# Norms' sums of squares, a positional term and weight low parts change engines in a two-layer decoder trunk

## The chip, the core and the metric

One core of a Trainium2 chip runs the whole program. The metric is device time in microseconds (us), the median of several executions. The engines are TensorE (PE for matmuls, PEld for its weight loads), VectorE (DVE), ScalarE (ACT), GpSimd (POOL) and SyncE (SP), whose queue issues the DMAs. Each has its own in-order queue, and semaphores order them.

## The reference

Two decoder layers on 256 tokens of width 1024, float32 throughout. Layer 0 mixes tokens by native sparse attention ("nsa"), layer 1 by differential attention ("diff").

```
for layer in (0, 1):
    x = x + 0.5 * swiglu(rmsnorm(x, ffn1_norm), ffn1_w_in, ffn1_w_out)      # 1024 -> 2 x 2816 -> 1024
    x = x + mixer(rmsnorm(x, mix_norm))                                     # 0: nsa, 1: diff
    x = x + 0.5 * swiglu(rmsnorm(x, ffn2_norm), ffn2_w_in, ffn2_w_out)
rmsnorm(x, g) = x * rsqrt(mean(x * x) + 1e-6) * g
# in nsa: overlapping blocks of 32 tokens, stride 16, become one token each through an MLP
blocks = concat(sub[:, :, 0:15], sub[:, :, 1:16])                           # sub: 16 tokens x 64 per head
kc, vc = gelu((blocks + pos) @ w1) @ w2                                     # pos: 32 x 64, for kc and for vc
# in diff: two softmaxes of one head are subtracted, p0 - lambda * p1, and multiply v
```

## The kernel before

Every product of float32 numbers is made of three TensorE products: both factors are split into a high part (a rounded copy) and a low part (the number less its high part), and high x high, high x low and low x high are summed in PSUM (`mm3`, `mm3x`; in the FFN one matmul of 512 columns and one of 256). Activations lie transposed, channels in partitions, in `xT`.

The weights come through the class `Stream`. A list of chunks of 128 x 2048 numbers (1 MB) is loaded in the order of use into three raw buffers by SyncE (`_load`); `_piece` splits 512 columns at a time: ScalarE writes the high part (L86), then VectorE (L89), GpSimd (L91) or both write the low part. `Stream.pool` is the share of each piece's low part that goes to GpSimd. It is 0 in the FFNs, `NSA_SPLIT` = 0.875 in the head loop of nsa (448 of 512 columns), `DIFF_SPLIT` = 1 in the head loop of diff and `TAIL_SPLIT` = 1 just after it. `pump` splits ahead of use, by at most two chunks.

`Norm` makes what the next stage multiplies with. For each of four banks, `parts` writes the scaled high and low parts `xhl` (L327 on ScalarE, L328 on VectorE), and `squares` squares the bank on ScalarE (L334) and adds it into `acc` on GpSimd (L336, and L338 for the last fold). `rms_row` (the FFNs) multiplies `acc` with a matrix of ones on TensorE (L352), which gives every partition the sum over channels, and takes the reciprocal root on VectorE in eight steps over 256 columns. `rms` (the mixers) does it with two columns. In the first FFN `rms_row` stands after the last k step of block 0, and the evacuation `evac(0)` (the SwiGLU product, split into `hh` and `hl`) after step 3 of block 1; in the other FFNs they stand after steps 6 and 1.

In `nsa`, the projection "kc" leaves compressed keys and values in two banks, tokens in partitions. ScalarE scales them into `kcn` and writes each twice side by side (L627). During the next projection `kc_t` transposes them four heads at a time (L637), and VectorE copies each bank out in two halves of 64 partitions while it adds the positional term (L641), which lies as a column per partition in `gcol`. Then `kcs` is the split of `kc2`, and `mlp` multiplies with it (L680, L682) in between the steps of the projection "q0".

In `diff`, the head loop runs eight heads two ahead: `qk` (L1075), `chain` (the biased scores on VectorE, L548, and the exponential on ScalarE, L549; the bias is made on GpSimd, L1062), `mid` (L1095 to L1102 on VectorE: the two softmaxes are normalised and subtracted) and `tr` (the transposes of the result, L1109). Between them `fill` hands out steps of a generator, `filler`: the projections dk1, dq1, dv0 and dv1, the products with v of the first heads (`pv`), a norm of each pair of heads (`sub_b`: L992 to L1007) and half of the output projection. How many steps stand where is written out in `DIFF_FILL`. The order of the instructions on each engine is set by a scheduler when the program is built, from priorities in the order of the source and a table of costs; `tc.high_priority` lifts the lines under it. The order on the chip is therefore not the order of the source in detail.

Of the kernel before, what the change touches and what calls it, by code (L numbers as in the profile page):

```python
# [10 lines left out]
F32 = mybir.dt.float32  # L11
# [6 lines left out]
P = 128  # L18
# [105 lines left out]
def trunk_kernel(ctx, tc, x, ffn1_norm, ffn1_w_in, ffn1_w_out, mix_norm, ffn2_norm, ffn2_w_in, ffn2_w_out,  # L124
# [38 lines left out]
    rows_b = t3("rows_b", P)[:40]  # L163
# [90 lines left out]
    def setup_late():  # L254
        for i, g in enumerate((mix_norm, ffn2_norm)):
            nc.sync.dma_start(rows_a[16 + 16 * i:32 + 16 * i, :], g.rearrange("l (k p) -> (l k) p", p=P))
        nc.sync.dma_start(cst[:, P:], consts[:, P:])
        for c in range(2):
            cs = slice(c * DH, (c + 1) * DH)
            nc.sync.dma_start(rows_b[0:1, cs], nsa_q_norm)  # L260
            nc.sync.dma_start(rows_b[1:4, cs], nsa_k_norm[0])
            nc.sync.dma_start(rows_b[4:5, cs], diff_q_norm)
            nc.sync.dma_start(rows_b[5:6, cs], diff_k_norm)
            for kv in range(2):
                nc.sync.dma_start(rows_b[8 + 16 * kv:24 + 16 * kv, cs], nsa_cmp_pos[0, kv, 16 * c:16 * c + 16, :])
        nc.sync.dma_start(rows_b[6:7, :], diff_subln)
        nc.sync.dma_start(rows_b[7:8, :], diff_subln)
        nc.sync.dma_start(w2sb, nsa_cmp_w2[0].rearrange("v (c p) d -> p v c d", p=P))

    def setup_late2(b):  # L270
        nc.tensor.transpose(b[:, :48], rows_a, ident[:48, :48])
        nc.vector.tensor_copy(gcol[:, 16:48], b[:, 16:48])
        nc.tensor.transpose(b[:, 64:104], rows_b, ident[:40, :40])
        nc.vector.tensor_copy(gcol[:, 48:88], b[:, 64:104])
# [3 lines left out]

    posT = gcol[:, 56:88].rearrange("p (v i) -> p v i", v=2)
# [31 lines left out]
    class Norm:  # L311
# [19 lines left out]
        def squares(self, b):  # L331
            xb = xT[:, 2 * b:2 * b + 2, :].rearrange("p k t -> p (k t)")
            sq = self.acc if b == 0 else t2("sq")
            nc.scalar.activation(sq, xb, AF.Square)  # L334
            if b:
                nc.gpsimd.tensor_tensor(self.acc, self.acc, sq, op=ALU.add)  # L336
            if b == 3:
                nc.gpsimd.tensor_tensor(self.acc[:, :S], self.acc[:, :S], self.acc[:, S:], op=ALU.add)  # L338

        def rms(self, ps):  # L340
# [7 lines left out]
            rsqrt(v, 2, self.r)  # L348

# [23 lines left out]
    def ffn(nrm, nxt_g, last=False, first=False):  # L373
# [7 lines left out]
        def stage1(p):  # L381
            for half in range(2):
# [3 lines left out]
                for kk in range(4):  # L386
# [13 lines left out]
                    if p == 0 and k == (7 if first else 6):  # L400
                        nrm.rms_row(B[2])
                    if p == 1 and k == (3 if first else 1):
                        evac(0)
# [210 lines left out]
    DIFF_FILL = [(2, 5), (2, 6), (1, 3), (1, 3), (1, 3), (1, 3), (1, 1), (1, 0)]  # L614
    NSA_SPLIT = 0.875
    DIFF_SPLIT = 1.0
    TAIL_SPLIT = 1.0

    def nsa(nrm, nxt_g):
# [6 lines left out]
        for tb in range(2):  # L626
            nc.scalar.activation(kcn[:, tb], halves(B[4 + tb], 8).unsqueeze(2).to_broadcast([P, 8, 2, DH]), AF.Copy,  # L627
                                 scale=r[:, tb:tb + 1])
# [5 lines left out]
        def kc_t(kv, tb):  # L634
# [5 lines left out]
            for rows, o0, o1, n0 in ((slice(0, DH), 8 * tb, 8 * tb + 8, 0), (slice(DH, P), 8 * tb - tb, 7 + 8 * tb, 1 - tb)):  # L640
                nc.vector.tensor_tensor(dst[rows, :, o0:o1], src[rows, :, n0:n0 + o1 - o0],  # L641
                                        posT[rows, kv, None, None, :].to_broadcast([DH, HKV, o1 - o0, 16]), op=ALU.add)
# [96 lines left out]
        for k in proj("q0", nrm, full(0), (4, 4)):  # L739
            next(m)  # L740
# [198 lines left out]
    def diff(nrm, nxt_g):  # L939
# [82 lines left out]
        def filler():  # L1022
# [14 lines left out]
            for k in proj("dv1", nrm, full(2), (4, 4)):  # L1037
                if k in (2, 5):
                    pv(k // 3, B[k // 3])
                if k in (4, 7):  # L1040
                    next(subs[k // 6])
                yield
            v_ev(1, 2)
            for g in subs:
                next(g)
# [80 lines left out]
        for h in range(2):  # L1126
            qk(h)
            chain(h)
            fill(2)
# [38 lines left out]
    for b in range(4):  # L1168
# [4 lines left out]
        nrm.parts(b, halves(B[b], 2))  # L1173
        W.pump(1, 512)
    W.pump(4, 512)
    for b in range(4):
        nc.vector.tensor_copy(xT[:, 2 * b:2 * b + 2, :].rearrange("p k t -> p (k t)"), B[b])
        nrm.squares(b)
# [36 lines left out]
```

## Time and profile before

| | us |
|---|---|
| median of 3 executions (1073.1 to 1074.43) | 1073.56 |
| the profiled execution, device time | 1074.49 |
| its span, first to last instruction | 1072.5 |
| PE busy in the span | 1040.3 (97%) |
| DVE busy | 797.1 (74%) |
| ACT busy | 615.5 (57%) |
| POOL busy | 143.1 (13%) |

Each stage shows in the profile as a stretch: the first FFN to about 202 us, nsa to 380, two FFNs to 757, diff to 890, the last FFN to the end. A wait is shown with what ended it ("<-"), and the idle time of an engine that is not the bound costs nothing.

### The profile page before, as it was taken

The numbers are of one execution on the slowest core, as the hardware profiler recorded it, in microseconds if no ns is written. First come the engines' busy times: TensorE is split into PE (matmuls) and PEld (weight loads), VectorE is DVE, ScalarE is ACT, GpSimd is POOL, SyncE is SP. The second block draws the span as 40 slices with busy tenths as digits, with TensorE's granted clock in tenths as the row PEclk, the third lists the DMA queues.
The fourth block names the chain that finished last, engine by engine and source line by source line (L and its number), as shares of the span: only waits on it lengthen the run. The fifth ranks groups of instructions, "written<-read, shape, count | busy, mean of one in ns | idle before, by whom it ended". The sixth has DMA issues, their size and how long they took to land.

```text
span 1072.5 us, 17582 instructions
## 1 busy us (share of the span) xinstructions
PE 1040.3 (97%) x6486; PEld 915.2 (85%) x6486; DVE 797.1 (74%) x1762; ACT 615.5 (57%) x1397; POOL 143.1 (13%) x168
## 2 busy tenths in 40 slices
PE   8999999989899999999999999999979899999998
PEld 6899999879676899999999999999857698888887
DVE  7876766889797796766779676677987867676674
ACT  6564555658487665555566455556647556565552
POOL 2000000100544010000000000001268542000000
PEclk9999999999899999999999999999989899999999
DMA  7756555378410266565565655546533435556551
GB/s 239 242 171 211 178 194 196 120 157 252 147 41 1 79 197 212 178 200 190 164 197 162 212 179 194 194 160 202 159 116 101 136 93 183 196 162 217 185 183 39
DMA packets 129970, 178.02 MB, mean 166 GB/s; under 512 B 5162, under 2 KB 104668, under 8 KB 129884
## 3 DMA queue, kind: packets, MB, share of 16 engines
q1 hardware_dynamic: 129708, 176.84, 51.4%
q8 instruction: 50, 0.82, 0.3%
q14 instruction: 36, 0.29, 0.1%
q10 hardware_dynamic: 176, 0.07, 0.0%
HBM read 175.84 MB, written 1.05 MB: 165 GB/s over the span
## 4 chain that ended last, share of the span: by engine, by line
PE 84%; DVE 10%; ACT 2%; issue 2%; DMA 1%; POOL 0%; SPq 0%; DVEq 0%; ACTq 0%; POOLq 0%
PE bank L396 27%; PE bank L398 14%; PE bank L359 7%; PE bank L360 6%; PE bank L361 6%; PE bank L364 6%; PE bank L365 6%; PE bank L366 6%; DVE wlo L89 3%; PE bank L920 1%; PE bank L901 1%; DVE kc L641 1%; DMA xnat<-in_x_dram 1%; PE bank L1075 1%; ACT p L549 1%
## 5 line engine op out<-in xcount | busy, mean ns | idle before, releaser
L89 DVE TENSOR_TENSOR wlo<-raw,whi 128x512 fp32r<-128x512 f32 (+1 forms) x623 | 402.2, 686 | 129.8 <-ACT whi L86 128.7
L86 ACT CAST whi<-raw 128x512 fp32r<-128x512 f32 x667 | 373.2, 618 | 200.8 <-PE bank L396 121.8
L396 PE MATMUL bank<-xhl,whi 128*128 128x512 f32 x1280 | 451.1, 394 | 0.0
L398 PE MATMUL bank<-xhl,wlo 128*128 128x256 f32 x1280 | 361.5, 282 | 0.0
L396 PEld LDWEIGHTS bank<-xhl,whi 128*128 128x128 f32 x1280 | 240.5, 188 | 54.1 <-DVE ab L418 0.2
L398 PEld LDWEIGHTS bank<-xhl,wlo 128*128 128x128 f32 x1280 | 240.7, 188 | 0.4
L364 PE MATMUL bank<-hh,whi 128*128 128x256 f32 x528 | 149.4, 283 | 1.1 <-ACT hh L424 1.1
L365 PE MATMUL bank<-hh,wlo 128*128 128x256 f32 x528 | 149.3, 283 | 0.0
L366 PE MATMUL bank<-hl,whi 128*128 128x256 f32 x528 | 149.2, 283 | 0.0
L416 DVE TENSOR_TENSOR ab<-bank,sh 128x256 f32<-128x256 f32 x160 | 60.2, 417 | 72.9 <-ACT sh L415 72.9
L415 ACT COPY sh<-bank 128x256 f32<-128x256 f32 x160 | 55.9, 374 | 94.3 <-PE bank L398 94.2
L336 POOL TENSOR_TENSOR acc<-acc,sq 128x512 f32<-128x512 f32 x18 | 28.6, 1590 | 596.7 <-ACT sq L334 596.0
L364 PEld LDWEIGHTS bank<-hh,whi 128*128 128x128 f32 x528 | 101.0, 191 | 2.6 <-ACT hh L424 1.4
L365 PEld LDWEIGHTS bank<-hh,wlo 128*128 128x128 f32 x528 | 101.0, 191 | 0.0
L366 PEld LDWEIGHTS bank<-hl,whi 128*128 128x128 f32 x528 | 101.0, 191 | 0.0
L91 POOL TENSOR_TENSOR wlo<-raw,whi 128x512 fp32r<-128x512 f32 (+1 forms) x60 | 75.5, 1286 | 110.9 <-ACT whi L86 108.4
L359 PE MATMUL bank<-whi,xhl 128*128 128x512 f32 (+1 forms) x192 | 77.4, 403 | 0.0
L360 PE MATMUL bank<-wlo,xhl 128*128 128x512 f32 (+1 forms) x192 | 75.4, 393 | 0.0
L361 PE MATMUL bank<-whi,xhl 128*128 128x512 f32 (+1 forms) x192 | 74.6, 389 | 0.0
L418 DVE TENSOR_TENSOR ab<-ab,rb 128x512 f32<-128x512 f32 x80 | 54.5, 681 | 0.0
L549 ACT ACTIVATE p<-p,mn 128x128 f32<-128x128 f32 (+1 forms) x96 | 42.9, 451 | 18.6 <-DVE mn L548 18.4
L424 ACT CAST hh<-sh 128x256 fp32r<-128x256 f32 x88 | 34.9, 399 | 19.4 <-DVE sh L422 19.4
(249 smaller groups left out, 1438.4 us busy)
## 6 DMA issues: line engine op xcount, KB each, us to landing
raw<-in_ffn_w_in_dram SPq DMA_DIRECT2D x174, 512.0 KB, 4.9
raw<-in_ffn_w_out_dram SPq DMA_DIRECT2D x44, 1024.0 KB, 5.0
raw<-in_diff_w_in_dram SPq DMA_DIRECT2D x12, 1024.0 KB, 5.2
raw<-in_nsa_w_in_dram SPq DMA_DIRECT2D x6, 1024.0 KB, 6.0
raw<-in_nsa_cmp_w_dram SPq DMA_DIRECT2D x8, 512.0 KB, 5.2
raw<-in_nsa_w_out_dram SPq DMA_DIRECT2D x4, 1024.0 KB
raw<-in_diff_w_out_dram SPq DMA_DIRECT2D x4, 1024.0 KB, 5.1
raw<-in_nsa_w_in_dram SPq DMA_DIRECT2D x4, 512.0 KB
```

What stands on the lines that cost most here:

```text
L86: self.nc.scalar.copy(hi[:, a:b], raw[:, a:b])
L89: self.nc.vector.tensor_tensor(lo[:, a:m], raw[:, a:m], hi[:, a:m].bitcast(F32), op=ALU.subtract)
L91: self.nc.gpsimd.tensor_tensor(lo[:, m:b], raw[:, m:b], hi[:, m:b].bitcast(F32), op=ALU.subtract)
L359: nc.tensor.matmul(ps, wh, xh, start=start, stop=False, skip_group_check=True)
L360: nc.tensor.matmul(ps, wh, xl, start=False, stop=False, skip_group_check=True)
L361: nc.tensor.matmul(ps, wl, xh, start=False, stop=stop, skip_group_check=True)
L364: nc.tensor.matmul(ps, wh, xh, start=start, stop=False, skip_group_check=True)
L365: nc.tensor.matmul(ps, wl, xh, start=False, stop=False, skip_group_check=True)
L366: nc.tensor.matmul(ps, wh, xl, start=False, stop=stop, skip_group_check=True)
L396: nc.tensor.matmul(g, wh, nrm.both[:, k].rearrange("p c t -> p (c t)"), start=k == 0, stop=False, skip_group_check=True)
L398: nc.tensor.matmul(g[:, :S], wl, nrm.hi[:, k, :], start=False, stop=k == KT - 1, skip_group_check=True)
L416: nc.vector.tensor_tensor(ab[j][:, cs], g[:, :S], sh[j][:, cs], op=ALU.add)
```

## The change

Three things change. (1) `squares` adds on VectorE; in the first FFN, whose input arrives with tokens in partitions, ScalarE squares the input itself and sums along the row (`squares_nat`), VectorE takes the reciprocal root of two columns and writes it on the diagonal of a matrix (`rms_nat`), and TensorE spreads it with the ones (`row_nat`); that row and `evac(0)` then stand where they stand in the other FFNs. (2) The positional term is loaded with tokens in partitions, repeated eight times over 16 tokens (`posn`, eight DMAs in place of four), and is added as the bank is scaled, on VectorE; the copies out of the transposes add nothing, and of their two halves one is ScalarE's. (3) The three shares are 0, so that VectorE makes every low part. With it the places of filler steps move: `DIFF_FILL`, three steps instead of two after each of the first two heads, the order of `pv` and `sub_b` in dv1, and the steps of `mlp` in q0, which start one later.

```diff
+    posn = bp.tile([P, HQ, S], F32, tag="qT", bufs=1, name="posn")[:, 0].rearrange("p (v c d) -> p v c d", v=2, c=2)
...
-            for kv in range(2):
-                nc.sync.dma_start(rows_b[8 + 16 * kv:24 + 16 * kv, cs], nsa_cmp_pos[0, kv, 16 * c:16 * c + 16, :])
+        for n in range(P // 16):
+            nc.sync.dma_start(posn[16 * n:16 * n + 16].rearrange("l v c d -> l (v c) d"),
+                              nsa_cmp_pos[0].rearrange("v (c l) d -> l (v c) d", l=16))
...
             if b:
-                nc.gpsimd.tensor_tensor(self.acc, self.acc, sq, op=ALU.add)
+                nc.vector.tensor_tensor(self.acc, self.acc, sq, op=ALU.add)
             if b == 3:
-                nc.gpsimd.tensor_tensor(self.acc[:, :S], self.acc[:, :S], self.acc[:, S:], op=ALU.add)
+                nc.vector.tensor_tensor(self.acc[:, :S], self.acc[:, :S], self.acc[:, S:], op=ALU.add)
...
+        def squares_nat(self, src, half):
+            if half == 0:
+                self.ss = tiny("xss", 4)
+            for tb in range(2):
+                i = 2 * half + tb
+                nc.scalar.activation(t2("junk"), src[:, tb, half * 512:(half + 1) * 512], AF.Square, accum_out=self.ss[:, i:i + 1])
+        def rms_nat(self):
+            v = tiny("v", 2)
+            nc.vector.tensor_tensor(v, self.ss[:, 0:2], self.ss[:, 2:4], op=ALU.add)
+            nc.vector.tensor_scalar(v, v, -0.5 / D, -0.5 * EPS, op0=ALU.mult, op1=ALU.add)
+            r = rsqrt(v, 2)
+            self.diag = t2("diag", S)
+            for tb in range(2):
+                nc.vector.tensor_scalar(self.diag[:, tb * P:(tb + 1) * P], ident, r[:, tb:tb + 1], None, op0=ALU.mult)
+        def row_nat(self, ps):
+            nc.tensor.matmul(ps[:, :S], ones, self.diag, start=True, stop=True)
+            self.rb = xp.tile([P, S], F32, tag="rb", bufs=1, name=nm("rb"))
+            nc.vector.tensor_copy(self.rb, ps[:, :S])
...
-                    if p == 0 and k == (7 if first else 6):
-                        nrm.rms_row(B[2])
-                    if p == 1 and k == (3 if first else 1):
+                    if p == 0 and k == 6:
+                        (nrm.row_nat if first else nrm.rms_row)(B[2])
+                    if p == 1 and k == 1:
                         evac(0)
...
-    DIFF_FILL = [(2, 5), (2, 6), (1, 3), (1, 3), (1, 3), (1, 3), (1, 1), (1, 0)]
-    NSA_SPLIT = 0.875
-    DIFF_SPLIT = 1.0
-    TAIL_SPLIT = 1.0
+    DIFF_FILL = [(2, 4), (1, 4), (2, 2), (1, 3), (1, 3), (1, 3), (1, 1), (1, 0)]
+    NSA_SPLIT = 0
+    DIFF_SPLIT = 0
+    TAIL_SPLIT = 0
...
-        for tb in range(2):
-            nc.scalar.activation(kcn[:, tb], halves(B[4 + tb], 8).unsqueeze(2).to_broadcast([P, 8, 2, DH]), AF.Copy,
-                                 scale=r[:, tb:tb + 1])
+        for kv in range(2):
+            hs = slice(kv * HKV, (kv + 1) * HKV)
+            for tb in range(2):
+                for c in range(2):
+                    nc.vector.scalar_tensor_tensor(kcn[:, tb, hs, c, :], halves(B[4 + tb], 8)[:, hs, :], r[:, tb:tb + 1],
+                                                   posn[:, kv, None, c, :].to_broadcast([P, HKV, DH]), op0=ALU.mult, op1=ALU.add)
...
-                nc.vector.tensor_tensor(dst[rows, :, o0:o1], src[rows, :, n0:n0 + o1 - o0],
-                                        posT[rows, kv, None, None, :].to_broadcast([DH, HKV, o1 - o0, 16]), op=ALU.add)
+                (nc.scalar.copy if n0 != 0 or o0 < 8 * tb else nc.vector.tensor_copy)(dst[rows, :, o0:o1], src[rows, :, n0:n0 + o1 - o0])
...
         for k in proj("q0", nrm, full(0), (4, 4)):
-            next(m)
+            if k:
+                next(m)
+            if k == KT - 1:
+                next(m)
...
             for k in proj("dv1", nrm, full(2), (4, 4)):
+                if k in (1, 4):
+                    pv(k // 4, B[k // 4])
                 if k in (2, 5):
-                    pv(k // 3, B[k // 3])
-                if k in (4, 7):
-                    next(subs[k // 6])
+                    next(subs[k // 5])
+                if k == 6:
+                    next(subs[0])
                 yield
             v_ev(1, 2)
-            for g in subs:
-                next(g)
+            next(subs[1])
...
             chain(h)
-            fill(2)
+            fill(3)
         mid(0)
...
         nrm.parts(b, halves(B[b], 2))
+        if b % 2:
+            nrm.squares_nat(x_nat, b // 2)
         W.pump(1, 512)
+    nrm.rms_nat()
     W.pump(4, 512)
-    for b in range(4):
+    for b in (2, 0, 1, 3):
         nc.vector.tensor_copy(xT[:, 2 * b:2 * b + 2, :].rearrange("p k t -> p (k t)"), B[b])
-        nrm.squares(b)
```

The row block `rows_b` shrinks from 40 rows to 8 with it, and the copy of its transpose in `setup_late2` from 40 columns to 8.

## Rows read from the trace of the kernel before

**Rows 1.** The page, part 1: busy time, share of the span, instructions.
```profile
PE 1040.3 (97%) x6486; PEld 915.2 (85%) x6486; DVE 797.1 (74%) x1762; ACT 615.5 (57%) x1397; POOL 143.1 (13%) x168
```
**Rows 2.** Waits of PE, longest in total first: total us, times, longest.
```profile
PE bank L1109 <- DVE p L1102: 6.5, 2, 6.3
PE bank L352 <- POOL acc L338: 3.3, 2, 1.7
PE bank L722 <- DVE ck L713: 3.0, 1, 3.0
PE bank L359 <- DVE ol L1005: 2.3, 1, 2.3
...
PE bank L1002 <- DVE on L999: 1.7, 1, 1.7
...
PE bank L680 <- DVE kcs L645: 1.3, 1, 1.3
PE bank L364 <- ACT hh L424: 1.1, 1, 1.1
PE bank L682 <- DVE wlo L89: 0.9, 2, 0.6
PE bank L637 <- DVE kc L641: 0.7, 1, 0.7
```
**Rows 3.** Stretches: us, busy us of PE, PEld, DVE, ACT, POOL; granted clock; DMA.
```profile
60.00:202.00 142.00, 142.00 (x946) 130.60 (x945) 96.00 (x189) 75.49 (x164) 0.00 (x0) 1.00 0.57 185
770.00:850.00 80.00, 69.50 (x340) 51.91 (x338) 66.79 (x167) 46.57 (x122) 57.59 (x67) 0.95 0.38 119
850.00:890.00 40.00, 39.65 (x304) 37.97 (x303) 28.77 (x69) 21.32 (x46) 18.53 (x13) 0.92 0.35 113
```
**Rows 4.** The same view, short stretches behind the two long waits of diff.
```profile
790.00:795.00 5.00, 5.00 (x14) 3.92 (x13) 2.44 (x3) 3.46 (x7) 1.68 (x2) 0.54 0.51 189
...
850.00:855.00 5.00, 4.94 (x19) 3.66 (x17) 4.70 (x13) 0.46 (x2) 1.67 (x2) 0.50 0.40 119
```
**Rows 5.** Timelines of DVE, POOL and PE, 764 to 800: start, us, instruction.
```profile
782.85 5.63 DVE L1100 TENSOR_SCALAR p<-p,f 128x128 f32<-128x128 f32 x2
...
799.21 0.28 DVE L1100 TENSOR_SCALAR p<-p,f 128x128 f32<-128x128 f32 x1
...
783.20 4.94 POOL L91 TENSOR_TENSOR wlo<-raw,whi 128x512 fp32r<-128x512 f32 x4
...
782.01 0.39 PE L360 MATMUL bank<-wlo,xhl 128*128 128x512 f32 x1
782.24 0.39 PE L361 MATMUL bank<-whi,xhl 128*128 128x512 f32 x1
788.91 0.89 PE L1109 MATMUL bank<-cst,p 128*128 128x128 f32 x2 [6.28 <-DVE p L1102]
```
**Rows 6.** Groups by line and form, DVE and POOL, 770 to 890: count, busy us, mean ns.
```profile
L1100 DVE TENSOR_SCALAR p<-p,f 128x128 f32<-128x128 f32 x8 | 9.6, 1202 | 0.1
L89 DVE TENSOR_TENSOR wlo<-raw,whi 128x512 fp32r<-128x512 f32 x12 | 8.0, 714 | 0.0
...
L306 DVE TENSOR_TENSOR ra<-ra,dv 128x4 f32<-128x4 f32 x4 | 2.7, 666 | 0.0
...
L91 POOL TENSOR_TENSOR wlo<-raw,whi 128x512 fp32r<-128x512 f32 x44 | 56.0, 1303 | 46.9 <-ACT whi L86 46.8
```
**Rows 7.** The same view over the whole span.
```profile
L91 POOL TENSOR_TENSOR wlo<-raw,whi 128x448 fp32r<-128x448 f32 x16 | 19.5, 1240 | 64.0 <-ACT whi L86 61.6 <-ACT oh L922 2.4
...
L641 DVE TENSOR_TENSOR kc<-bank,gcol 64x512 f32<-64x512 f32 x6 | 6.4, 1072 | 0.1
...
L328 DVE SCALAR_TENSOR_TENSOR xhl<-bank,gcol,xhl 128x256 fp32r<-128x256 f32 x8 | 3.8, 480 | 1.6 <-ACT xhl L327 1.4
```
**Rows 8.** Timelines of DVE at the start and of POOL at 886.
```profile
19.49 8.47 DVE L89 TENSOR_TENSOR wlo<-raw,whi 128x512 fp32r<-128x512 f32 x8
...
886.09 5.12 POOL L336 TENSOR_TENSOR acc<-acc,sq 128x512 f32<-128x512 f32 x1 [2.89 <-ACT sq L334]
```

More of the change, by code (lines that the diff above doesn't have):

```diff
@@ L162, in trunk_kernel @@
     rows_a = t3("rows_a", P)[:48]
-    rows_b = t3("rows_b", P)[:40]
+    rows_b = t3("rows_b", P)[:8]
+    posn = bp.tile([P, HQ, S], F32, tag="qT", bufs=1, name="posn")[:, 0].rearrange("p (v c d) -> p v c d", v=2, c=2)
     gcol = cp.tile([P, 96], F32, name="gcol")
@@ L272, in setup_late2 @@
         nc.vector.tensor_copy(gcol[:, 16:48], b[:, 16:48])
-        nc.tensor.transpose(b[:, 64:104], rows_b, ident[:40, :40])
-        nc.vector.tensor_copy(gcol[:, 48:88], b[:, 64:104])
+        nc.tensor.transpose(b[:, 64:72], rows_b, ident[:8, :8])
+        nc.vector.tensor_copy(gcol[:, 48:56], b[:, 64:72])
         nc.vector.tensor_scalar(gk[:, :3], gcol[:, 49:52], gcol[:, 48:49], -0.125, op0=ALU.mult, op1=ALU.mult)
@@ L277, in setup_late2 @@
         nc.vector.tensor_scalar(gsub, gcol[:, 54:55], 1.0 - lam_init, None, op0=ALU.mult)
-    posT = gcol[:, 56:88].rearrange("p (v i) -> p v i", v=2)
     def load_lambda():
```

## The prediction

> **What bounds the kernel now.** I read the shares of busy time first. TensorE is busy for 97% of the span [rows 1], and in the FFNs without a gap: 142.00 of 142.00 us in the stretch from 60 to 202, with VectorE at 96 and GpSimd at 0 [rows 3]. The change leaves TensorE's work as it is, so nothing can be won there. What can be won is the 32.2 us in which TensorE isn't busy (1072.5 less 1040.3), and the time in which it runs at its lower clock. So the second view is what TensorE waited for, longest in total [rows 2]. Three families stand out: waits for `acc` from GpSimd (3.3 us), waits around the compression in nsa (L637, L680, L682: 2.9 us), and waits in the head loop of diff (L1109, L1002, L359: 10.5 us). The third view is the stretches: from 770 to 850 TensorE lacks 10.5 of 80 us while GpSimd is busy for 57.59 [rows 3]. Just behind the two long gaps of diff the granted clock is 0.54 and 0.50, the lower of its two levels, 1.2 of 2.4 GHz [rows 4]. With 5 us each that is (1 - 0.54) x 5 + (1 - 0.50) x 5 = 4.8 us more.
>
> The fourth view, the timeline, tells why. VectorE started a pair of L1100 at 782.85 and needed 5.63 us; a single one of the same form took 0.28 us at 799.21. In those 5.63 us GpSimd ran four low parts back to back, 783.20 to 788.14, and TensorE's transposes started at 788.91, right behind [rows 5]. So the VectorE instruction was held while GpSimd worked, and TensorE paid 6.28 us for it. The groups of 770 to 890 show it as a rule: L1100 takes 1202 ns in the mean, and L306, four numbers per partition, 666 [rows 6]. It goes the other way too: one GpSimd addition took 5.12 us at 886 [rows 8].
>
> **The change part by part.**
>
> *Low parts to VectorE in diff.* 44 pieces leave GpSimd (56.0 us) [rows 6]. On VectorE one costs 8.0/12 = 0.67 us, or a little less where pieces follow each other and overlap; with 0.62, 44 x 0.62 = 27.3 us. Against it stands what VectorE no longer loses. L1100 alone loses 9.6 - 8 x 0.28 = 7.4 us [rows 5, 6]. Nineteen groups of that stretch, from L1100 (128x128) to L306, are stretched in the same way; at the shortest time of each form they lose about 33 us together. GpSimd keeps what is not L91, mostly biases: 57.59 + 18.53 - 56.0 = 20 us, a quarter of its time there [rows 3, 6]. So I take 27 of the 33 as won; the bounds are 10 and 33. The additions of the norm bring 3 x 0.67 + 0.4 = 2.4 us. VectorE's load from 770 to 890 is then 66.79 + 28.77 + 27.3 + 2.4 - 27 = 98 us, about what it was.
>
> What happens to the gap at 782? The four pieces that GpSimd ran there, and four before them, are 8 x 0.62 = 5 us on VectorE ahead of the chain; the stretched steps before 782 and VectorE's idle moments pay for most of that. L1100 itself gets 5 us shorter, so L1102 should end near 785. TensorE reaches the transposes later: two more filler steps stand ahead of them, of six matmuls of 512 columns, 0.23 us apart [rows 5], 2.8 us together, so near 785.3. I leave 0.5 of 6.5 us (bounds 0 and 3). The waits at L1002 and L359 (4.0 us) come from `sub_b`, a row of tiny steps stretched like L306, and `dv1` now starts it earlier. I leave 1.0 of 4.0. With the gaps the low clock behind them goes (4.8). Since VectorE is loaded for 98 us in a stage of some 106, some head will wait that doesn't now: I add 2.0 (bounds 0 and 10). Sum: -(6.5 + 4.0 + 4.8) + 0.5 + 1.0 + 2.0 = -11.8 us.
>
> *Low parts in nsa.* 16 pieces of 448 columns [rows 7] go to VectorE, where 16 stumps of 64 columns become full pieces: below 16 x 0.67 = 11 us, and VectorE loses stretching there too. The wait for L722 (3.0 us) sits on a chain of small steps that the low parts stretch and delay; four of them were GpSimd's and now stand in VectorE's queue at that place. I count 0; bounds -7 (with the low clock behind it, taken as in diff) and +2.
>
> *Sums of squares.* On GpSimd an addition takes up to 5.12 us [rows 8], on VectorE 0.67. At the start the sum now comes from the input itself, no longer through copies, squares, three additions and a fold: half of the 3.3 us goes. VectorE gets some 12 tiny steps ahead of the low parts of the second chunk, at an estimated 0.2 us (L306 without its stretching) 2.5 us. Against that, eight low parts took 8.47 us there beside GpSimd's additions, where 8 x 0.62 is 5 [rows 8], and eight steps of 256 columns disappear. ScalarE's squares move into its pause before the last half of the input; the second pair may push its first weight pieces by under a microsecond. With `evac(0)` two steps earlier the wait for `hh` (1.1 us) goes. In the last FFN the wait for `acc`, the other half of 3.3, goes: its last addition needed those 5.12 us. At the other norms no wait stands; VectorE's adds there are paid for by an unstretched L328. Sum: -(3.3 + 1.1) = -4.4 us, bounds -4.4 and -2.
>
> *Positional term.* VectorE gains 8 instructions of 128 x 256 out of PSUM, 480 ns by the nearest row (L328, bank) [rows 7], about 3.5 us in a row, in part in idle time. It loses 8 x 1.07 us (L641) and gets four copies of half the partitions. These cost between 0.67 (a plain piece of 512 columns) and 1.07 us (L641, if the strided write is what is slow) [rows 6, 7]; I take 0.9, between them. ScalarE loses two instructions and gets the other four copies. The two halves then run side by side, so `kcs` is ready before TensorE gets there, all the more as the first step of `mlp` starts one step of q0 later: the 1.3 goes, and the 0.9. The first bank is freed no earlier than now, since the eight scalings stand before it; I leave the 0.7 [rows 2]. Gain 2.2 us, bounds 0 and 2.9. Eight DMAs instead of four pass SyncE's queue in the third block of the first FFN, among the weight loads. Three raw buffers give those loads a lead of two chunks, which hides them; without it TensorE would wait for the four, a microsecond or two.
>
> **The skill against the trace.** VectorE was held for a run of four GpSimd instructions [rows 5]. The Trainium skill ("SBUF — State Buffer", "SBUF: two separate sides") says that the two engines share a pair of ports as an exclusive lock, which the first to start keeps for its whole instruction. Taken by the letter, a hold lasts one instruction; that is rival F. Another page speaks against the change: the Trainium skill, "Perfetto Trace Analysis", "Optimizing Scalar/DVE Operations", lets a saturated VectorE offload work, even to GpSimd, though it warns that between these two it may not help. That is rival B.
>
> **How the numbers follow.** -11.8 - 4.4 - 2.2 = -18.4 us. Against the profiled execution, 1074.49 us, that is 1056.1; the median of the runs, 1073.56, is 0.9 us lower, so 1055.2: I say 1055.
>
> A. *Forecast*, 1050 to 1059: 47%.
>
> B. *VectorE becomes the bound, slower.* Place: the head loop of diff. If the long L1100 and L306 aren't GpSimd's doing, VectorE has 24.4 us idle from 770 to 890 [rows 3] and gets 27.3 + 2.4: at least 5 us more, and each of eight heads waits behind two pieces, 1.2 us, another 10. The gaps of diff stay; 6.6 us are won elsewhere: 1073.6 + 15 - 6.6 = 1082. It decides if less than a third of the 33 us comes back. For it: 98 of 106 us even by my count. Against: rows 5. 6%.
>
> C. *New waits eat half.* VectorE's order puts pieces before the chain, or GpSimd's biases are now held by VectorE's runs, as the addition at 886 was: one more us at each of eight heads and one more stretch at the low clock, 8 + 2.4: 1065. 20%.
>
> D. *The wait for L722 goes as well*, with its low clock, 7 us: 1048. 17%.
>
> E. *The gaps only move* under the scheduler's new order: 1073. 5%.
>
> F. *GpSimd holds VectorE for one instruction only*, 4.94/4 = 1.24 us; the rest of the 6.28 has another cause and stays, 1055.2 + 6.28 - 1.24 - 0.5 = 1059.7: 5%. Against it: four instructions fill the hold to the end.
>
> Faster by more than 0.2% (2.1 us, about what a measurement of this kernel tells from none): A, C, D and F, 0.89; within it E, 0.05; slower B, 0.06. The range takes in A, C, D and F and the bounds of the new waits: 1044 to 1067.
>
> **What would show it.** After the change L1100 (128x128) should take about 0.3 us and L306 0.2; no wait of TensorE for `acc`; the wait for L1102 under 1 us; no stretch at half clock in the head loop of diff; VectorE at about 0.9 there; L91 gone. If L1100 stays above 0.9 us, the mechanism is wrong. If it shrinks and TensorE still lacks 10 us in diff, it is C.

## The result, and the profile after

The changed kernel takes 1048.18 us (median of four executions, 1047.14 to 1048.75) against 1073.33 us of the kernel before beside it: ratio 0.9765, 95% interval 0.9748 to 0.9782. That is 25 us faster, inside the predicted range, 7 us below the predicted 1055, and the time that rival D gave (1048). The profiled execution took 1047.14 us in all, with a span of 1045.4.

The page of the kernel after, part 1, answers [rows 1].

```profile
PE 1028.2 (98%) x6486; PEld 906.8 (87%) x6486; DVE 779.2 (75%) x1834; ACT 618.4 (59%) x1403; POOL 39.5 (4%) x84
```

TensorE has the same 6486 matmuls, and yet is busy for 12.1 us less (1040.3 before). That is the clock: its mean granted value was 0.987 in the profiled execution before and is 1.000 after. The time in which TensorE isn't busy fell from 32.2 to 17.2 us, by 15.0. The two sum to the 27.1 us between the spans. VectorE took over 60 low parts and is busy for 18 us *less*, standing still included. With the low parts alone moved it is 8 less (789.2 us, run e1 below), and with the other steps alone also 18 less (779.1, run e2).

TensorE's waits after, longest in total first (total us, times, longest), answer [rows 2]. In the new source L1139 is the old L1109, L1132 the old L1102, L1130 the old L1100, L383 to L385 the old L359 to L361, L748 the old L722.

```profile
PE bank L1201 <- DMA xnat<-in_x_dram: 3.1, 2, 2.7
PE bank L1194 <- DVE warm L1192: 1.6, 1, 1.6
PE bank L1139 <- DVE p L1132: 1.3, 1, 1.3
PE bank L894 <- DVE mn L572: 1.1, 1, 1.1
PE bank L383 <- ACT oh L1033: 0.8, 1, 0.8
```

The waits for `acc`, `ck` and `kcs` are gone, and of the wait for L1102 in diff 1.3 is left of 6.5. The longest wait is now for the input itself, which no step of the change touches.

To see where the time went, I cut both spans at the same TensorE instructions: the first matmul of block 1 of the first FFN, the first transpose of `kcn`, the first matmul of the second FFN's block 1, the first `qk` of diff and the first block-1 matmul of the last FFN. Stretches of the kernel before, then of the kernel after (length, busy us of PE, PEld, DVE, ACT, POOL, granted clock, DMA): start, rest of the first FFN, nsa, diff.

```profile
0.00:25.40 25.40, 20.16 (x119) 16.58 (x120) 17.64 (x27) 17.26 (x33) 6.08 (x10) 0.93 0.79 251
25.40:221.91 196.51, 195.40 (x1255) 177.35 (x1254) 142.74 (x284) 109.20 (x234) 5.29 (x5) 1.00 0.60 187
221.91:383.38 161.47, 151.95 (x991) 124.79 (x989) 137.46 (x424) 107.78 (x289) 44.11 (x65) 0.97 0.37 110
774.89:894.83 119.94, 107.48 (x641) 89.06 (x641) 93.65 (x235) 64.30 (x160) 74.20 (x77) 0.94 0.38 122
```

```profile
0.00:22.00 22.00, 17.29 (x117) 14.58 (x118) 15.10 (x38) 14.21 (x31) 0.51 (x6) 1.00 0.85 280
22.00:217.16 195.16, 195.16 (x1257) 177.51 (x1256) 141.99 (x290) 110.84 (x239) 0.44 (x1) 1.00 0.61 192
217.16:370.09 152.93, 146.88 (x990) 121.25 (x989) 131.05 (x424) 111.25 (x292) 21.17 (x45) 1.00 0.39 115
761.61:867.50 105.89, 103.56 (x641) 86.04 (x641) 87.10 (x276) 64.56 (x160) 17.36 (x32) 1.00 0.40 130
```

Each row splits into busy time (the same matmuls, so what falls there is the clock, give or take the two matmuls that changed sides in the first rows) and the rest, the gaps:

| stretch | gained | of it gaps | of it TensorE's busy time |
|---|---|---|---|
| start | 3.4 | 0.5 | 2.9 |
| rest of first FFN | 1.4 | 1.1 | 0.2 |
| nsa | 8.5 | 3.5 | 5.1 |
| diff | 14.1 | 10.1 | 3.9 |
| all else | -0.2 | -0.2 | 0.0 |

The stretch of diff reaches into the last FFN, so that one of the two waits for `acc` (1.6 us at 892 in the kernel before) is among its gaps.

VectorE's forms in the stretch 770 to 890 of the kernel after (count, busy us, mean ns), which answer [rows 6]:

```profile
L89 DVE TENSOR_TENSOR wlo<-raw,whi 128x512 fp32r<-128x512 f32 x64 | 42.4, 688 | 3.0 <-ACT whi L86 3.0
L1132 DVE SCALAR_TENSOR_TENSOR p<-p,f 128x256 f32<-128x256 f32 x8 | 3.9, 489 | 0.0
L1130 DVE TENSOR_SCALAR p<-p,f 128x128 f32<-128x128 f32 x8 | 2.3, 283 | 0.1
L306 DVE TENSOR_TENSOR ra<-ra,dv 128x4 f32<-128x4 f32 x4 | 0.6, 156 | 0.0
```

L1130 takes 283 ns where it took 1202 (eight instructions of 9.6 us in all, of which a single one took 5.37), and the tiny step L306 156 where it took 666 (`rsqrt`, L300 to L308, has the same lines in both kernels).

### The profile page after: what moved, and what is told of

It is laid out like the page before. It is cut to its first block, busy times and chain, and to the rows that moved or that the text cites. A ratio compares the mean times of both kernels' runs of the same rounds, so it can differ in the third digit from the quotient of the medians.

```text
span 1045.4 us, 17560 instructions
## 1 busy us (share of the span) xinstructions
PE 1028.2 (98%) x6486; PEld 906.8 (87%) x6486; DVE 779.2 (75%) x1834; ACT 618.4 (59%) x1403; POOL 39.5 (4%) x84
## 4 chain that ended last, share of the span: by engine, by line
PE 90%; DVE 4%; ACT 3%; DMA 1%; issue 1%; SPq 0%; POOL 0%; ACTq 0%; POOLq 0%
PE bank L420 28%; PE bank L422 15%; PE bank L383 7%; PE bank L384 7%; PE bank L385 7%; PE bank L388 6%; PE bank L389 6%; PE bank L390 6%; DVE wlo L89 2%; PE bank L949 2%; ACT p L573 1%; PE bank L930 1%; PE bank L1105 1%; ACT whi L86 1%; DMA xnat<-in_x_dram 1%
## 5 line engine op out<-in xcount | busy, mean ns | idle before, releaser
L89 DVE TENSOR_TENSOR wlo<-raw,whi 128x512 fp32r<-128x512 f32 x667 | 432.4, 685 | 133.7 <-ACT whi L86 132.4
L383 PE MATMUL bank<-whi,xhl 128*128 128x512 f32 (+2 forms) x192 | 75.2, 392 | 0.1
L384 PE MATMUL bank<-wlo,xhl 128*128 128x512 f32 (+2 forms) x192 | 72.9, 380 | 0.7 <-DVE wlo L89 0.7
L385 PE MATMUL bank<-whi,xhl 128*128 128x512 f32 (+2 forms) x192 | 72.9, 381 | 0.0
L572 DVE CUSTOM_DVE_ANT_0 p<-bank,bias,fac 128x128 f32<-128x128 f32 (+1 forms) x96 | 36.6, 409 | 9.2 <-PE bank L1105 6.8
L384 PEld LDWEIGHTS bank<-wlo,xhl 128*128 128x128 f32 x192 | 36.2, 189 | 7.6 <-DVE wlo L89 1.1
```

Of the source, the lines that this page charges most:

```text
L89: self.nc.vector.tensor_tensor(lo[:, a:m], raw[:, a:m], hi[:, a:m].bitcast(F32), op=ALU.subtract)
L383: nc.tensor.matmul(ps, wh, xh, start=start, stop=False, skip_group_check=True)
L384: nc.tensor.matmul(ps, wh, xl, start=False, stop=False, skip_group_check=True)
L385: nc.tensor.matmul(ps, wl, xh, start=False, stop=stop, skip_group_check=True)
```

## The experiments

The theory: what cost the time before is that a VectorE instruction stands still while GpSimd works on SBUF. Rivals: that GpSimd's low parts came late, that the new order of diff is what won, and F, that a hold lasts one GpSimd instruction only. Times of runs on different chips are compared through their ratio to the kernel before beside them; 0.001 is 1.07 us, and the intervals are given.

**The shares alone** (e1), in the kernel before:

```
-    NSA_SPLIT = 0.875
-    DIFF_SPLIT = 1.0
-    TAIL_SPLIT = 1.0
+    NSA_SPLIT = 0
+    DIFF_SPLIT = 0
+    TAIL_SPLIT = 0
```

> The kernel before with one thing changed: VectorE makes all the low parts in nsa's loop, in diff's loop and behind it; order of the filler, sums of squares and positional term stay. Theory (GpSimd's instructions hold VectorE's): the gap ahead of the transposes of diff, the wait for L722 in nsa and the half clock behind both go, L1100 takes about 0.3 us: 1056 us (1052 to 1061). Rival (the new order of the filler and of sub_b is what won): 1068 to 1073.

Measured: 1058.74 us, ratio 0.9874 (0.9857 to 0.9891): 13.5 of the 25.2 us come with three numbers. No wait for L722 appears in the profile, and the longest wait for L1102 is 1.5 us. Not all low clock in nsa is gone: behind a new wait of 2.9 us for `mn` (L865) the granted clock is 0.66 from 285 to 290.

**The shares put back** (e2), in the kernel after: the same lines the other way round.

> The kernel after with GpSimd's shares of the low parts put back (0.875 in nsa, all in diff and behind it), all else as after. Theory (GpSimd holds VectorE): the pairs of subtractions that were L1100 take 1.2 us in the mean again, the waits for L1102 and L722 come back: 1065 us (1060 to 1070). Rival (order): 1048 to 1052.

Measured: 1069.98 us, ratio 0.9966 (0.9942 to 0.9990), ten executions between 1063.67 and 1074.07. Their times follow the mean granted clock, from 0.992 in the fastest to 0.980 in the two slowest. The waits for L1132 (6.0 us, longest 4.3) and for `ck` (3.5) are back. L1130 takes 429 ns in the mean, not the 1.2 us that I expected: the long hold of [rows 5] didn't come back. So in the kernel after the shares are worth 21.6 us by the medians, and 15.5 by the fastest execution of this run. The rival of the order is out with these two runs, and with this one:

**The order of diff as before** (e6), in the kernel after:

```
-    DIFF_FILL = [(2, 4), (1, 4), (2, 2), (1, 3), (1, 3), (1, 3), (1, 1), (1, 0)]
+    DIFF_FILL = [(2, 5), (2, 6), (1, 3), (1, 3), (1, 3), (1, 3), (1, 1), (1, 0)]
...
-            fill(3)
+            fill(2)
...   # and pv, sub_b in dv1 at their old steps
```

> The kernel after with the order of diff as before: old table of filler steps, two steps ahead of the first mid, old places of pv and sub_b in dv1. Theory (the shares won diff, the order only a rest): the diff stage is as long as in the run with the shares alone, 109.4 us against 105.9 from the first qk to the last FFN: 1051 to 1052.5. Rival (order and shares need each other): 1058 or more. Rival (order is worth nothing): 1048.

Measured: 1047.62 us, ratio 0.9757 (0.9742 to 0.9771), not to be told from the kernel after. My own expectation was wrong and the last rival right: the order is worth nothing that this can show. Diff is 107.79 us long in its profile, 105.89 after; if something is left of the order there, the times don't show it.

**Diff's share alone put back** (e9): `DIFF_SPLIT` and `TAIL_SPLIT` 1.0, nsa as after.

> The kernel after with GpSimd's low parts put back in diff and behind it only, nsa as after. Theory: of the 21.8 us that both shares cost, nsa's part is 4 to 7 (the wait for L748 of 3.5 us, and what follows), diff's the rest: 1063 to 1066. Rival (nsa's share costs nothing): 1070.

Measured: 1060.34 us, ratio 0.9876 (0.9860 to 0.9892): 11.9 us more than after, less than expected. Its timeline shows the mechanism best. GpSimd and VectorE from 776, as the first heads' `mid` begins (start us, us, instruction, count):

```profile
776.54 5.17 POOL L91 TENSOR_TENSOR wlo<-raw,whi 128x512 fp32r<-128x512 f32 x4
```

```profile
776.53 0.16 DVE L307 SCALAR_TENSOR_TENSOR ra<-ra 128x16 f32<-128x16 f32 x1
776.61 1.35 DVE L1132 SCALAR_TENSOR_TENSOR p<-p,f 128x128 f32<-128x128 f32 x1
777.88 1.23 DVE L308 SCALAR_TENSOR_TENSOR ry<-ra,ry 128x16 f32<-128x16 f32 x1
779.04 1.55 DVE L1132 SCALAR_TENSOR_TENSOR p<-p,f 128x256 f32<-128x256 f32 x1
780.51 1.37 DVE L541 TENSOR_SCALAR ry<-ry,rcol 128x8 f32<-128x8 f32 x2
```

The same stretch of the kernel after, in which GpSimd makes no low parts:

```profile
776.27 0.17 DVE L307 SCALAR_TENSOR_TENSOR ra<-ra 128x16 f32<-128x16 f32 x1
776.36 0.34 DVE L1132 SCALAR_TENSOR_TENSOR p<-p,f 128x128 f32<-128x128 f32 x1
776.62 0.17 DVE L308 SCALAR_TENSOR_TENSOR ry<-ra,ry 128x16 f32<-128x16 f32 x1
776.70 0.48 DVE L1132 SCALAR_TENSOR_TENSOR p<-p,f 128x256 f32<-128x256 f32 x1
777.10 0.36 DVE L541 TENSOR_SCALAR ry<-ry,rcol 128x8 f32<-128x8 f32 x2
```

Four VectorE steps in a row meet four GpSimd instructions, and each is held through one of them: from the first L1132 to the end of L541 it is 5.3 us where it was 1.1. Small steps suffer most: 128 x 16 numbers take 1.23 us instead of 0.17.

**nsa's share alone put back** (e8): `NSA_SPLIT` 0.875, diff as after.

> The kernel after with GpSimd's share of 0.875 of the low parts in nsa's loop put back, diff as after. Theory (the share in nsa was the cause of the wait for ck, of 3 us, and of the half clock behind it, and stretched the qk loop): the run with both shares less the run with diff's alone, 9.6 us, comes back here: 1055 to 1058.5. Rival (the wait for ck went with the positional term and the share is worth what the forecast said, nothing): 1048 to 1050.

Measured: 1053.14 us, ratio 0.9821 (0.9806 to 0.9836): 6.0 us more than after. It falls between my two expectations, and the rival "worth nothing" is out. One wait of TensorE, and the stretch behind it at the lower of TensorE's two levels:

```profile
PE bank L748 <- DVE ck L739: 3.4, 1, 3.4
```

```profile
275.00:280.00 5.00, 5.00 (x20) 4.68 (x21) 1.55 (x4) 1.35 (x3) 0.66 (x1) 0.50 0.00 0
```

VectorE and GpSimd on the way to that `ck`, in the same run:

```profile
263.53 4.96 POOL L91 TENSOR_TENSOR wlo<-raw,whi 128x448 fp32r<-128x448 f32 x4 [60.74 <-ACT whi L86]
```

```profile
264.28 3.19 DVE L89 TENSOR_TENSOR wlo<-raw,whi 128x512 fp32r<-128x512 f32 x3
267.39 0.14 DVE L736 TENSOR_SCALAR cv<-css 64x1 f32<-64x1 f32 x1
267.45 1.12 DVE L89 TENSOR_TENSOR wlo<-raw,whi 128x64 fp32r<-128x64 f32 x1
...
268.56 0.20 DVE L89 TENSOR_TENSOR wlo<-raw,whi 128x64 fp32r<-128x64 f32 x1
```

The share left VectorE a stump of 64 columns per piece. The row of three holds one whole piece and two stumps; the four stumps of this chunk by their form, from 263 to 272:

```profile
L89 DVE TENSOR_TENSOR wlo<-raw,whi 128x64 fp32r<-128x64 f32 x4 | 3.6, 924 | 0.0
```

Three of them took 1.12 to 1.19 us beside GpSimd, the last 0.20 without it. VectorE spent more on such a stump than the 0.69 us that the whole piece costs it. The same place in the kernel after:

```profile
262.88 1.28 DVE L89 TENSOR_TENSOR wlo<-raw,whi 128x512 fp32r<-128x512 f32 x2
264.08 0.14 DVE L736 TENSOR_SCALAR cv<-css 64x1 f32<-64x1 f32 x1
```

From the end of the second MLP product (L732's copy) to the transpose of `ck` it is 8.0 us here and 6.4 after (264.07 to 272.03; 262.68 to 269.04). The difference lies ahead of L736: from the copy to it 3.3 us here, with the whole piece and the two held stumps between, and 1.4 after. In this run nsa is 5.2 us longer than after, of which 1.7 is gaps and 3.6 TensorE's busy time.

**The positional term back** (e7): loaded into `rows_b`, `posT` from `gcol`, ScalarE scales into `kcn`, VectorE adds out of the transposes, as before the change; the rest, the later first step of `mlp` among it, as after.

```
-                (nc.scalar.copy if n0 != 0 or o0 < 8 * tb else nc.vector.tensor_copy)(dst[rows, :, o0:o1], src[rows, :, n0:n0 + o1 - o0])
+                nc.vector.tensor_tensor(dst[rows, :, o0:o1], src[rows, :, n0:n0 + o1 - o0],
+                                        posT[rows, kv, None, None, :].to_broadcast([DH, HKV, o1 - o0, 16]), op=ALU.add)
```

> The kernel after with the positional term added after the transposes as before, from gcol, and its four DMAs; mlp's first step stays one step later. Theory (the term's move wins the stretch from the last kc_t to ck): 3 to 4 us back there, 1051 to 1053. Rival (that stretch was won by the shares in nsa): 1048 to 1049.

Measured: 1050.41 us, ratio 0.9790 (0.9766 to 0.9813): 2.7 us more than after by the medians, though the intervals overlap. In the profile the way from the first transpose of `kcn` to the first matmul of L892, the first head's `qk` (L894 in the kernel after), is 58.7 us, after 56.0. The wait for `ck` doesn't come back: that one belongs to the share. TensorE's next wait in the head loop is twice as long as the 1.1 us after:

```profile
PE bank L892 <- DVE mn L572: 2.3, 1, 2.3
```

**The squares' additions alone** (e5), in the kernel before:

```
-                nc.gpsimd.tensor_tensor(self.acc, self.acc, sq, op=ALU.add)
+                nc.vector.tensor_tensor(self.acc, self.acc, sq, op=ALU.add)
...   # and the fold
```

> The kernel before, its squares' additions and the fold made on VectorE and no more. Theory: TensorE's two waits for acc (3.2 us) shrink to the length of VectorE's own additions, and nothing else moves: 1070 to 1071.5. Rival (the additions only wait in VectorE's queue, or an acc wait is replaced by one for the next thing): 1073 to 1074.

Measured: 1069.51 us, ratio 0.9960 (0.9945 to 0.9974): 4.3 us won, a little more than expected. No wait for `acc` is left; in their place the first FFN waits 2.0 us for `ab` (L396).

**A second subtraction on GpSimd that nobody waits for** (e3), in the kernel after. Nothing is left out; the extra results go to a scratch.

```
+            if self.pool:
+                for c in range(a, b, 512):
+                    e = min(b, c + 512)
+                    self.nc.gpsimd.tensor_tensor(self.scr[:, c - a:e - a], raw[:, c:e], hi[:, c:e].bitcast(F32), op=ALU.subtract)
```

> The kernel after, in which VectorE makes all low parts, but GpSimd subtracts each of the 44 pieces of diff a second time into a scratch that nobody reads. Nothing waits for these values. Theory (GpSimd's instruction holds VectorE's for as long as it lasts): VectorE, at 99 us from 770 to 890, loses 25 to 33 us more, the pairs of L1100 take 1 us in the mean: 1060 to 1072. Rival (what cost time before was only that GpSimd's low parts came late): 1048 to 1050.

Measured: 1078.99 us, ratio 1.0067 (1.0048 to 1.0086): 32 us slower than after, slower than the kernel before, and beyond my 1072. The rival "only late low parts" is out: no low part comes from GpSimd here. The extra instructions also keep their raw buffers longer (four loads waited for one of them, 15.1 us in all on SyncE's queue), but no wait of TensorE in diff is for a weight; the long ones are for VectorE's results, L1134 (6.8 us) and L1036 (4.8) first. VectorE and GpSimd in the head loop:

```profile
802.83 0.68 DVE L89 TENSOR_TENSOR wlo<-raw,whi 128x512 fp32r<-128x512 f32 x1
803.43 1.25 DVE L305 TENSOR_TENSOR ra<-ra,qv 128x16 f32<-128x16 f32 x1
804.61 0.68 DVE L89 TENSOR_TENSOR wlo<-raw,whi 128x512 fp32r<-128x512 f32 x1
805.21 1.27 DVE L306 SCALAR_TENSOR_TENSOR fac<-ra,fac 128x16 f32<-128x16 f32 x1
806.40 0.68 DVE L89 TENSOR_TENSOR wlo<-raw,whi 128x512 fp32r<-128x512 f32 x1
807.00 1.26 DVE L307 SCALAR_TENSOR_TENSOR ra<-fac 128x16 f32<-128x16 f32 x1
```

```profile
800.21 8.03 POOL L93 TENSOR_TENSOR scr<-raw,whi 128x512 f32<-128x512 f32 x5 [6.89 <-issue]
```

The engines take turns: one VectorE instruction runs while GpSimd waits (GpSimd's own come to 1.6 us each here), the next is held while GpSimd works. Forms of VectorE from 770 to 890 in this run:

```profile
L1134 DVE SCALAR_TENSOR_TENSOR p<-p,f 128x256 f32<-128x256 f32 x8 | 7.5, 939 | 0.0
L574 DVE CUSTOM_DVE_ANT_0 p<-bank,bias,fac 128x128 f32<-128x128 f32 x14 | 4.8, 342 | 4.0 <-PE bank L1107 4.0
L1051 DVE COPY oraw<-bank 128x512 f32<-128x512 f32 x4 | 2.7, 680 | 0.0
```

L1134 (L1132 in the kernel after) takes 939 ns where 489 stood, but the forms that read a bank are as long as without the extra work. One detail of my expectation missed: the 128x128 scalings (L1132 here, L1130 in the kernel after) grew only from 283 to 422 ns in the mean; the low parts, at 891, and the subtractions behind the scalings took most of the holds. Diff is 141.08 us long, 35.2 more than after: 19.0 us more gaps, and 16.2 more busy time of TensorE at a granted clock of 0.84.

**The same in quarters** (e4): `range(a, b, 128)`.

> As the run with the second subtraction, but in four instructions of 128 columns each (176 instead of 44). Theory (a VectorE instruction is held through a run of GpSimd instructions): same as that run or somewhat slower, 1060 to 1075, and the pairs of L1100 still near 1 us. Rival F (held for one instruction only): a hold is a quarter as long, the pairs take below 0.6 us, 1050 to 1055.

Measured: 1075.44 us, ratio 1.0026 (1.0016 to 1.0036). The same place in the timeline:

```profile
802.85 0.43 DVE L305 TENSOR_TENSOR ra<-ra,qv 128x16 f32<-128x16 f32 x1
803.20 0.68 DVE L89 TENSOR_TENSOR wlo<-raw,whi 128x512 fp32r<-128x512 f32 x1
803.80 0.43 DVE L306 SCALAR_TENSOR_TENSOR fac<-ra,fac 128x16 f32<-128x16 f32 x1
```

Neither theory came out whole. A hold is shorter, 0.43 us for the tiny step, as F says: it lasts one GpSimd instruction. But the time hardly falls, since the holds become more: from 757 to 890 I count 115 VectorE instructions that are over 0.1 us longer than their form is in the kernel after, by 27 us in all, where run e3 has 43, by 33 us. Quarters are also longer in sum (an instruction of 128 columns takes 565 ns in the mean, so four take 2.3 us), and VectorE waits about 4 us for GpSimd, whose biases queue behind them, so that the time isn't a clean measure of the holds.

**One input, and none** (e10, e11, e12). In place of the second subtraction GpSimd copies the raw piece times one; or writes zeros; or writes zeros three times per piece, tied to the piece by one column that ScalarE writes first:

```
+                self.nc.scalar.copy(self.scr[:, :1], raw[:, a:a + 1])
+                for _ in range(3):
+                    self.nc.gpsimd.memset(self.scr[:, :b - a], 0.0)
```

> The kernel after, in which GpSimd, beside each of the 44 low parts that VectorE makes in diff, copies the piece's raw weights times one into a scratch that nobody reads: one input where the run with the second subtraction had two. Theory (any GpSimd instruction that reads and writes SBUF holds VectorE's that have all operands there): pairs of subtractions, tiny steps and low parts of VectorE are stretched as in that run, by the length of GpSimd's instruction: 1060 to 1078. Rival (only GpSimd's two inputs hold): 1048 to 1052.

> As the run before, but GpSimd writes zeros into the scratch, 44 times 128x512, and reads nothing. Theory of the plain lock (any GpSimd instruction holds): all VectorE forms with their operands in SBUF are stretched, 1055 to 1070. Rival, by the Trainium skill (SBUF - State Buffer, SBUF: two separate sides): forms with two SBUF inputs (L89, L304, L305) conflict only with a GpSimd instruction that reads, so they stay at 0.69 and 0.17 us and at most the forms with one input (L302, L1131) are stretched: 1048 to 1054.

> The memsets of the run before fell into the end of nsa, since nothing bound them. Here ScalarE writes one column of the scratch ahead of each of the 44 pieces, so that GpSimd's memsets (three of 0.53 us per piece, about as long as a subtraction) come beside that piece's low part in diff. Theory (a GpSimd instruction that reads nothing from SBUF holds no VectorE instruction): pairs and low parts unstretched, 1047 to 1050, of which up to 2 are for the 44 short ScalarE steps. Rival (any GpSimd instruction holds VectorE forms with operands in SBUF): 132 x up to 0.5 us of holds, 1058 to 1075. Between (only forms with one input, as L1130, are held): L89 at 0.69, L1130 at 0.6 or more, 1050 to 1056.

Measured for the copy: 1066.74 us, ratio 0.9930 (0.9903 to 0.9957), five executions from 1060.33 to 1067.69. The copies are longer than the subtractions (1634 ns), but a hold is short: of some 89 VectorE instructions with operands in SBUF that started within one, some 27 were held, none by more than 0.46 us. So the time lies in the range of my theory, and the theory's length of a hold is wrong. Of the time, 4.0 us is one wait of VectorE for a bias behind the copies in GpSimd's queue; how the rest of the 17.7 us over the kernel after divides isn't shown. Measured for the zeros without a tie: 1046.98 us, ratio 0.9766 (0.9750 to 0.9782). As nothing bound them, they ran from 352 to 378 us, ahead of diff, so the time tests nothing; the run is a miss in its construction.

Measured for the tied zeros: 1061.26 us, ratio 0.9894 (0.9875 to 0.9912), outside what my theory gave and in the range of the rival. But the 13.8 us over the kernel after can't be put down to holds: ScalarE's one column waits for the memsets of the piece before. Forms of the stretch 757 to 890, ScalarE's last:

```profile
L89 DVE TENSOR_TENSOR wlo<-raw,whi 128x512 fp32r<-128x512 f32 x62 | 40.9, 687 | 4.6 <-ACT whi L86 4.4
L1132 DVE TENSOR_SCALAR p<-p,f 128x128 f32<-128x128 f32 x8 | 3.7, 460 | 0.1
L1134 DVE SCALAR_TENSOR_TENSOR p<-p,f 128x128 f32<-128x128 f32 x8 | 2.7, 341 | 0.0
L91 ACT COPY scr<-raw 128x1 f32<-128x1 f32 x41 | 7.8, 191 | 26.0 <-POOL scr L93 26.0
```

So of the time I claim nothing. Of the forms, the expectation in between came nearest: beside an instruction of GpSimd that reads nothing, VectorE's forms with two inputs in SBUF (L89, L1134) run at full speed, and the form with one (L1132) is still held, 460 ns in the mean against 283. Of the instructions that started within a memset, some 15 of 21 with one input were held, and 2 of some 42 with two.

No version of these beats the kernel after by more than the measurement can tell.

## Why the prediction was right, and where it was off

The sum was 18.4 us, the gain 25.2. Term by term, with the runs that undo or do one part:

| part | predicted | measured |
|---|---|---|
| low parts in diff | -11.8 | -11.9 (e9 against after) |
| low parts in nsa | 0, bounds -7 and +2 | -6.0 (e8 against after) |
| sums of squares | -4.4 | -4.3 (e5: the additions alone) |
| positional term | -2.2 | -2.7 (e7 against after; the intervals overlap) |

The third row agrees in part by luck: the predicted 4.4 holds 1.1 us for the earlier `evac(0)`, which e5 doesn't have, and of the 6.6 us between the spans of before and e5 only 2.8 are gaps; 3.8 are TensorE's busy time (1040.3 and 1036.5), and the sum had no clock in that term.

**The step that failed** is "I count 0" for nsa. The wait for L722 is the share's doing, and the prediction had its mechanism in hand (small steps that low parts stretch and delay) but set against it that four pieces would now stand in VectorE's queue at that place. They do stand there, and they are cheap: 0.68 us each and nothing held, while with the share a stump took up to 1.19 us for an eighth of the columns (run e8). Rival D said it: the wait goes, with its clock. It priced the two at 7; the run with the share back gives 6.0.

**The second term that was mis-sized is the clock.** The sum took 4.8 us for it, all in diff. The table of stretches shows 12.1: 3.9 in diff, 5.1 in nsa, 2.9 at the start. In nsa two stretches of the kernel before, right behind the wait for `ck`, were at 0.50 and 0.56:

```profile
280.00:285.00 5.00, 5.00 (x22) 4.71 (x22) 2.66 (x5) 2.10 (x4) 4.38 (x4) 0.50 0.01 4
285.00:290.00 5.00, 5.00 (x15) 3.91 (x15) 4.08 (x19) 1.86 (x7) 0.59 (x3) 0.56 0.52 158
```

The start isn't the change's: there the granted clock from 10 to 15 us was 0.71 before and 1.00 after, but between 0.66 and 0.74 in the runs e4, e8, e10 and e12, which have the start of the kernel after, and 1.00 in e5, whose input comes in as before. That part of what the profiles show is luck; how much of it the medians hold can't be read from them. By gaps alone the forecast was 13.6 us (18.4 less 4.8), and 15.0 were measured.

**Diff came out as worked out**, though not through each row. The wait for L1102 went from 6.5 to 1.3, not quite below 1; the waits behind `sub_b` left 0.8 us for `oh` instead of the 1.0 I had left; the gaps of the stage fell by 10.1 us, 8.5 without the wait for `acc`, where the sum had 7.0 and kept 2.0 for new waits that didn't come; no stretch of it is below full clock. VectorE is busy for 87.1 of 105.9 us, a share of 0.82, where I had said 0.9, and did not become the bound: rival B is out. Of the 33 us of stretching, I had taken 27 as won. Summing each VectorE instruction's time over the time that its form takes undisturbed, from the timelines of 770 to 890 before and after, I get about 35 and 2 us; it moves by a few us with what is taken as undisturbed.

**What I misread** is the hold itself. Four GpSimd instructions held one VectorE instruction in [rows 5] (the first of the pair, 5.37 us by itself), and I took that for the rule against F. It is the exception. It also makes up more than half of the 9.6 us behind the mean of 1202 ns, which I read as a rule: the other seven took 0.6 us in the mean, four of them 0.28 or 0.29. In the kernel before, 34 VectorE instructions of the forms that can be held started within an L91, at least 0.25 us ahead of its end. 33 of them were held, and ended with that L91 or less than 0.6 us behind its end; the other one, 0.02 us behind its L91, ran through. Only the one of [rows 5], which had started 0.35 us ahead of the four, lasted through all of them, and in the runs e2, e8 and e9, which have the shares back, no held instruction lasts 2 us. Why that one did stays open. F is right on a single hold. Its price, 1059.7, was wrong, since a chain of steps pays one hold for each: run e9 shows four in a row. The Trainium skill ("SBUF — State Buffer", "SBUF: two separate sides") says that whichever starts first keeps the shared ports for its whole instruction; those 33 agree, and the one of [rows 5] doesn't.

**The start** gained what was said of the waits and lost it elsewhere: the wait for `acc` (one of the two in [rows 2]) is gone, and TensorE waits 3.1 us for the input instead of 2.0. This wait is between 0.7 and 2.7 us at its longest in the profiles of one and the same start, so it moves from execution to execution. The wait for `hh` went as said: the rest of the first FFN has no gap left, 195.16 of 195.16 us.

**Not settled:** with the order of diff worth nothing and the parts done alone, the measured terms sum to 24.9 of 25.2 us. But both shares together (e2) cost 21.6 us in the kernel after, with an interval of 2.6 to either side for e2 alone, where one by one they cost 17.9, and in the kernel before they cost 13.5 (e1). The 10 us between e2's executions go with their clock, and the three at 0.990 or more are 15.5 to 18.3 us above the kernel after, so that the surplus over 17.9 may be clock alone; whether the shares work on each other, I can't say. In e7 part of the loss is a clock of 0.54 from 280 to 285 us, right behind the wait of 2.3 us; behind the 1.1 us after it stayed at 1.00. At one mean clock, 0.998, two executions of e7 took 1049.72 and 1049.78 us and one of the kernel after 1048.41, so that by these few the term without its clock is worth about 1 of the 2.7 us. No run undoes alone the new start (`squares_nat` to `row_nat`, with the earlier `evac(0)`) or the later first step of `mlp`.

## What to carry to other kernels

Offloading elementwise work from VectorE to GpSimd can cost VectorE more than doing it: here VectorE made 60 pieces more and was busy for 8 us less (797.1 us before, 789.2 in e1), and in the kernel after it is as busy with them as without (779.2, and 779.1 in e2). Look for it in the profile by one form at two lengths (a tiny step at 0.16 and 1.23 us), and count the steps of a dependent chain that meet GpSimd's instructions, not GpSimd's busy share. When a wait goes, count the clock behind it too, in each stage where the short stretches show a low one: here that was 9.0 of the 27.1 us between the spans, in nsa and diff together.

## What the runs showed of the hardware that I had not expected

- Which forms are held. Beside GpSimd's subtraction (run e3) VectorE's TENSOR_TENSOR, SCALAR_TENSOR_TENSOR and TENSOR_SCALAR with all operands in SBUF are held to its end; forms that read a bank (L574 342 ns, L1051 680), reductions (L536: 681) and reciprocals (L1127: 166) are not.
- What GpSimd does matters. Two inputs (run e3): VectorE is held to the end of the instruction, by up to 1.1 us. One input (run e10, 1.6 us long): by 0.46 at most. No input (run e12): two-input forms of VectorE as good as never (L89 687 ns), one-input forms mostly, to the memset's end (0.53 us). The Trainium skill, in the section named above, says that forms with two SBUF inputs conflict only with a GpSimd instruction that reads SBUF; the memsets agree. The copies of run e10 do read it, and held such forms for 0.4 us of their 1.6 at most, not for the whole instruction; here the measurement decides.
- It goes both ways: GpSimd's second subtraction took 1471 ns in the mean from 766 to 890 in run e3, next to a busy VectorE, where its low parts took 1303 before.
